# A LoRA router on one core: trip counter instead of an address test, the logits' wrap once per trip, spare products at other places

## The chip, the core and the metric

The kernel runs on one NeuronCore of a Trainium2 chip. The metric is the device time of one execution in microseconds; the time before is the median of three runs. The profile is of a separate execution of the same program, and times inside it count from its first instruction.

## The reference

```python
batch, seq, dim, num_loras = 16, 512, 1024, 8      # x: 16 x 512 x 1024 fp32
logits = np.matmul(x, router_weights)              # router_weights: 1024 x 8
exp_logits = np.exp(logits - np.max(logits, axis=-1, keepdims=True))
out = exp_logits / np.sum(exp_logits, axis=-1, keepdims=True)
```

A matrix of 8192 rows and 1024 columns is multiplied by 1024 x 8 weights, and each row's eight logits go through a softmax. Input is 33.55 MB, output 0.26 MB.

## The kernel before

**Blocks.** The 8192 rows are taken as 128 partitions of 64 rows, and block j is row j of every partition, so 128 rows of 1024 values. `x_all` holds all 64 blocks in SBUF in bf16 and no place in it is used twice; so a load never waits for the compute engines.

**Loads.** `LOADS` (line 40) is the list of loads in blocks: one of 4, four of 8, four of 4, three of 2, five of 1, which makes 63. The first, blocks 0 to 3, is issued by SyncE as fp32 into `x_f32` and cast by ScalarE (line 361). The others are issued by GpSimd, one after another (line 187), and are cast on the way. The loads of eight bring blocks 4 to 11, 12 to 19, 20 to 27 and 28 to 35. Block 63 comes last, in three pieces of 512, 256 and 256 columns (line 200). SyncE waits for each load in turn and adds its number of blocks to one semaphore, `s_in` (lines 170 to 175).

**TensorE.** [...] each block is first turned: eight 128 x 128 transposes against an identity, five into the PSUM tile `ptv` and three into `pts` (line 296 in the profile, since `loop_turn` copies the instruction written there; two tiles of each, used in turn). VectorE copies `ptv` to `xTv` (line 421), ScalarE `pts` to `xTs` (line 375). Then eight matmuls with the turned block as stationary operand and the bf16 weights as moving operand (128 x 8) accumulate a block's logits in `lg` (line 283 in the profile, copied from the spare product). Turns run one block ahead of products.

The order on TensorE is written out by hand as a loop of its own (lines 305 to 324). One trip handles two blocks: `rows_turn` turns an odd block (`loop_turn(1)`) and multiplies the even one before it; `rows_even` turns the next even block (`loop_turn(0)`); `rows_multiply` runs two spare products and multiplies the odd block. A spare product (`fill`, line 283) multiplies a constant tile of 512 columns into a PSUM tile that nobody reads; it keeps the array occupied. Each turn begins with a wait for `s_in` (line 232), each product with a wait for both copies of its block, `s_c` (line 262).

**Registers.** Eight registers `r_x` hold the address of the next block's eight column groups, and `r_l` the address of the logits in PSUM, 256 bytes further with each block. The ring of logits has 16 places of 256 bytes, so the address wraps at 4096: line 246 clears that bit after each addition. After each turn the additions stand in two fused register operations with that line between them (lines 243, 246, 247 in the profile). At the end of `rows_turn` lines 319 and 320 decide if spare products are inserted: some bits of the address of the next block are compared, which holds for blocks 12, 20, 28 and 36; the address of `x_all` (`ROW_AT`, line 57) is chosen so that these bits fall right. If it holds, `rows_spare` runs six spare products ahead of the turn of that block. Line 323 ends the trip and branches back to `rows_multiply`.

**After the loop.** Blocks 61 and 62 are multiplied, block 63 is turned by pieces (`turn_piece`, lines 332 to 337, each with its own wait) and multiplied (lines 346 to 354). The softmax of blocks 0 to 59 runs by groups of eight on VectorE and ScalarE beside the loop, that of the last four one by one (lines 366, 470, 524 to 531). SyncE stores blocks 0 to 59 and then the last four.

## Time and profile before

| | |
|---|---|
| time, median of 3 (all) | 85.59 us (85.55 to 85.71) |
| span of the profiled execution | 84.5 us |
| TensorE matmul, busy | 69.4 us (82%) |
| VectorE / ScalarE, busy | 39.4 / 38.0 us |
| spare products, 85 | 25.8 us, 401 ns each |
| turns in the loop, `ptv` + `pts` | 29.0 + 21.7 us |
| products in the loop, `xTv` + `xTs` | 16.7 + 13.2 us |
| granted TensorE clock, mean | 0.994 |
| GpSimd's loads: packets, bytes, share of 16 engines' span | 2736, 15.73 MB, 90.2% |

Matmuls overlap in the array, so their durations add up to more than the time that passes: a transpose is recorded with some 218 ns, but the next one starts 55 ns later. The bytes of a queue are counted as written, in bf16. PEq is TensorE's sequencer, which works through register operations, branches and waits; where the array waits for one, the line behind `<-PEq` names it. Line 232 is the wait for loaded blocks.

### The profile page before, as it was taken

To read this page: it belongs to the slowest core of one execution; us is meant where nothing else is said; L and a number is where in the kernel's file an instruction comes from. 1 tells how busy PE (TensorE), PEld (TensorE's weight loads), DVE (VectorE), ACT (ScalarE), POOL (GpSimd) and SP (SyncE) were. 2 spreads that over 40 slices of the span, in tenths; PEclk is the share of its full clock that TensorE was granted. 3 is DMA by queue.
4 is the path that set the end of the run, shared out by engine and by line. 5 is a ranking of instruction groups with operands and counts; after the bars stand their busy time and mean duration, and the time that the engine had idled before them with its cause. 6 is when DMAs were issued, how large, how long until landed. Compare 5 with 4: busy or idle time off the path is not lost. (4 is left out here: it accounts for less than half of the span.)

```text
span 84.5 us, 3030 instructions
## 1 busy us (share of the span) xinstructions
PE 69.4 (82%) x1118; PEld 54.2 (64%) x1118; DVE 39.4 (47%) x114; ACT 38.0 (45%) x81; POOL 11.3 (13%) x26
## 2 busy tenths in 40 slices
PE   0070366779999999979996999999999999999870
PEld 0040455659786787638882787678877888877650
DVE  0030042224563476427551476437657646765662
ACT  0600968223354265425442265426556544655570
POOL 0699996000000000000000000000000000000000
PEclk9999999999999999999999999999999999999997
DMA  5999979997999799989997999999999999999930
GB/s 165 402 434 248 248 155 225 241 241 155 233 241 225 163 241 241 217 171 241 241 217 159 217 217 217 217 213 221 202 233 190 215 211 215 201 210 210 164 114 11
DMA packets 3184, 18.12 MB, mean 215 GB/s; under 512 B 488, under 2 KB 1000, under 8 KB 2032
## 3 DMA queue, kind: packets, MB, share of 16 engines
q0 software_dynamic: 2736, 15.73, 90.2%
q1 hardware_dynamic: 432, 2.36, 7.3%
q10 hardware_dynamic: 16, 0.03, 0.1%
HBM read 33.59 MB, written 0.26 MB: 401 GB/s over the span
## 5 line engine op out<-in xcount | busy, mean ns | idle before, releaser
L421 DVE COPY xTv<-ptv 128x640 bf16<-128x640 bf16 x63 | 31.0, 492 | 33.1 <-PE ptv L296 28.0
L375 ACT COPY xTs<-pts 128x384 bf16<-128x384 bf16 x63 | 30.0, 476 | 35.5 <-PE pts L296 35.1
L296 PE MATMUL ptv<-identity,x_all 128*128 128x128 bf16 x311 | 29.0, 226 | 7.6 <-PEq L232 4.1
L283 PE MATMUL spare<-filler 128*128 128x512 bf16 x85 | 25.8, 401 | 0.1
L296 PEld LDWEIGHTS ptv<-identity,x_all 128*128 (+1 forms) x311 | 19.1, 100 | 9.7 <-issue 9.2
L296 PE MATMUL pts<-identity,x_all 128*128 128x128 bf16 x186 | 21.7, 228 | 0.0
L283 PEld LDWEIGHTS lg<-w_bf,xTv 128*128 128x128 bf16 x305 | 15.8, 99 | 8.0 <-issue 1.6
L283 PE MATMUL lg<-w_bf,xTv 128*128 128x8 bf16 x305 | 16.7, 167 | 0.0
L296 PEld LDWEIGHTS pts<-identity,x_all 128*128 x186 | 13.9, 103 | 0.0
L283 PE MATMUL lg<-w_bf,xTs 128*128 128x8 bf16 x183 | 13.2, 166 | 0.0
L283 PEld LDWEIGHTS spare<-filler 128*128 128x128 bf16 x85 | 6.1, 101 | 4.8 <-issue 0.6
L283 PEld LDWEIGHTS lg<-w_bf,xTs 128*128 128x128 bf16 x183 | 9.0, 96 | 0.0
L187 POOL DMA_DIRECT2D x_all<-in_x_dram x16 | 8.6, 600 | 2.2 <-POOLq L149 2.2
L361 ACT CAST x_all<-x_f 128x1024 bf16<-128x1024 f32 x4 | 4.0, 1044 | 5.0 <-ACTq L378 5.0
L290 PE MATMUL lg<-ident,w 8*128 8x8 f32 x8 | 1.0, 250 | 4.7 <-PEq L288 4.7
L290 PEld LDWEIGHTS lg<-ident,w 8*128 8x128 f32 x8 | 0.9, 197 | 4.7 <-issue 4.7
L441 DVE TENSOR_REDUCE mx<-lg 128x8 f32 x8 | 1.8, 225 | 4.4 <-DVEq L491 4.0
L412 DVE CAST identity<-ident 128x128 bf16<-128x128 f32 x1 | 0.5, 518 | 4.6 <-POOL ident L193 4.6
L364 ACT ACTIVATE ev<-ex 128x64 f32<-128x64 f32 x8 | 2.0, 256 | 1.4 <-DVE ex L441 0.8
L377 ACT ACT_TABLE_LOAD x1 | 1.3, 1283 | 2.2 <-PEq L149 2.2
L457 DVE TENSOR_REDUCE ssum<-ev 128x8 f32<-128x64 f32 x8 | 1.7, 218 | 0.0
L441 DVE TENSOR_TENSOR ex<-lg,mx 128x64 f32<-128x64 f32 x8 | 1.7, 216 | 0.0
(41 smaller groups left out, 16.0 us busy)
## 6 DMA issues: line engine op xcount, KB each, us to landing
x_all<-in_x_dram POOLq DMA_DIRECT2D x4, 2048.0 KB, 27.7
x_all<-in_x_dram POOLq DMA_DIRECT2D x4, 1024.0 KB, 51.7
x_f<-in_x_dram SPq DMA_DIRECT2D x1, 2048.0 KB, 8.4
x_all<-in_x_dram POOLq DMA_DIRECT2D x3, 512.0 KB, 62.1
x_all<-in_x_dram POOLq DMA_DIRECT2D x5, 256.0 KB, 66.2
out_dram<-out_all SPq DMA_DIRECT2D x1, 240.0 KB, 2.0
x_all<-in_x_dram POOLq DMA_DIRECT2D x1, 128.0 KB, 67.8
x_all<-in_x_dram POOLq DMA_DIRECT2D x2, 64.0 KB, 67.6
```

What stands on the lines that cost most here:

```text
L187: nc.gpsimd.dma_start(out=xa[:, first[i]:first[i] + r, :], in_=x_rows[:, first[i]:first[i] + r, :]).then_inc(s_ld[i], 16)
L283: return pe.matmul(spare, lhsT=filler[:, 0:P], rhs=filler, start=True, stop=True)
L290: t = pe.transpose(w_ps[:, n, :], w8[:, :, n], ident[0:KO, 0:KO])
L296: turn_like = pe.transpose(turn_ap(0, 0), xa[:, 0, 0:P], identity).ins
L361: act.copy(xa[:, k, :], x_f32[:, k, :]).then_inc(s_cast, 1)
L364: return act.activation(ev, ex, func=Exp).then_inc(s_ev, 1)
L375: act.copy(xTs[j % 2], pts[j % 2][:, 0:SN, :]).then_inc(s_c[j % 2], 1)
L377: act.preload_act_table(Exp)
L412: dve.tensor_copy(out=identity, in_=ident).then_inc(s_idb, 1)
L421: dve.tensor_copy(out=xTv[j % 2], in_=ptv[j % 2][:, 0:VN, :]).then_inc(s_c[j % 2], 1)
L441: return dve.add_instruction(kind(name=f"I-{nc.next_id()}", engine=dve.engine, **k))
L457: dve.reduce_sum(ssum[:, :, 0], ev, axis=X).then_inc(s_d, 1)
```

## The change

The test of address bits makes way for a counter. `r_t` starts at 1 and goes down by one in each odd turn, in the same fused operation as the addresses; when it falls below 1, the new `rows_wait` adds four (half of the eight blocks of a large load), and a second test asks if the next block lies below block 36, the end of the loads of eight. If so, the spare products run; if not, `rows_last` sets the counter so high that it doesn't return. There are five spare products in a group instead of six. The logits' address is wrapped in odd turns alone: it starts at place 3, so in even turns it can't reach the end of the ring. As no address bits are tested any more, `x_all` moves to the start of the free space, and `x_f32` behind it.

The aim is fewer register operations on TensorE's sequencer per trip, and no spare products where the loads are small.

```diff
-    LOT, SPARE = 8, 6
-    ROW_AT = 32 - LOADS[0] - LOT
-    assert LOADS[1:5] == [LOT] * 4 and 64 - ROW_AT == LOADS[0] + LOT * 5
+    LOT, SPARE = 8, 5
+    LOTS = LOADS.count(LOT)
+    assert LOADS[1:1 + LOTS] == [LOT] * LOTS
...
+    X_AT = place[0]
+    xa = sb("x_all", [P, J, D], bf16)
     x_f32 = sb("x_f32", [P, LOADS[0], D], fp32)
-    place[0] = X_AT = ROW_AT * D * 2
-    xa = sb("x_all", [P, J, D], bf16)
...
     pe.reg_mov(r_l, LG_AT + 256 * (SKIP - 1))
+    pe.reg_mov(r_t, 1)
...
         pe.reg_add(r_l, r_l, 256)
+        if b == 1:
+            pe.reg_add(r_t, r_t, -1)
         for c in range(KO):
-            if c == KO // 2:
+
+            if c == KO // 2 and b == 1:
                 pe.reg_alu(r_l, r_l, -4097, ALU.bitwise_and)
             pe.reg_add(r_x[c], r_x[c], D * 2)
...
     nc.br("rows_turn", engines=only_pe)
+
+    with nc.body("rows_wait", valid_engines=only_pe):
+        pe.reg_add(r_t, r_t, LOT // 2)
+        pe.br_lt(
+            r_x[0], X_AT + D * 2 * (LOADS[0] + LOTS * LOT),
+            on_true="rows_spare", on_false="rows_last",
+        )
+    with nc.body("rows_last", valid_engines=only_pe):
+        pe.reg_mov(r_t, J)
+        pe.br("rows_even")
     with nc.body("rows_spare", valid_engines=only_pe):
         for _ in range(SPARE):
             fill()
...
         multiply(0, None)
-        pe.reg_alu(r_t, r_x[0], (64 + 32 + LOT - 1) * D * 2, ALU.bitwise_and)
-        pe.br_eq(r_t, 32 * D * 2, on_true="rows_spare", on_false="rows_even")
+        pe.br_lt(r_t, 1, on_true="rows_wait", on_false="rows_even")
```

## The prediction

> **What bounds the kernel now.** I read the page first: the slices and the traffic.

> ```profile
> PE   0070366779999999979996999999999999999870
> ...
> DMA  5999979997999799989997999999999999999930
> ...
> HBM read 33.59 MB, written 0.26 MB: 401 GB/s over the span
> ```

> Both rows are full for most of the span: the DMA engines from about 2 us to slice 37, TensorE from about 21 us on, and busy shares cannot tell which sets the end. The wait that does is found in the timeline of TensorE (start, length, line, what it does, idle before it):

> ```profile
> 35.03 1.45 PE L283 MATMUL spare<-filler 128*128 128x512 bf16 x6
> 36.93 0.44 PE L296 MATMUL ptv<-identity,x_all 128*128 128x128 bf16 x5 [0.45 <-PEq L232]
> ...
> 44.37 1.46 PE L283 MATMUL spare<-filler 128*128 128x512 bf16 x6
> 46.60 0.44 PE L296 MATMUL ptv<-identity,x_all 128*128 128x128 bf16 x5 [0.78 <-PEq L232]
> ...
> 54.04 1.46 PE L283 MATMUL spare<-filler 128*128 128x512 bf16 x6
> 55.33 0.44 PE L296 MATMUL ptv<-identity,x_all 128*128 128x128 bf16 x5
> ...
> 79.70 0.44 PE L296 MATMUL ptv<-identity,x_all 128*128 128x128 bf16 x5 [0.40 <-PEq L232]
> ```

> These are the waits of line 232, for data: 0.45 us ahead of block 20, 0.78 ahead of block 28, then none for 33 us, then 0.40 ahead of block 62, the last whole block. So TensorE runs behind the loads from 46.6 us and catches up with them only at the end. The other side of that wait is SyncE's line 175, which counts each landed load:

> ```profile
> L175 SPq EVENT_SEMAPHORE  x16: 17/17/17, 17.3 to 79.5; - x16
> ```

> Cut into windows, its records stand at 17.3, 27.0, 36.8, 46.4 (loads of eight), 51.3, 56.1, 61.1, 65.9 (fours), 68.3, 70.8, 73.3 (twos), then 74.5, 75.7, 77.0, 78.3 and 79.5. A load of eight reads 8 x 128 x 1024 x 4 B = 4.19 MB in 9.7 us, 433 GB/s; the rate is the same late in the kernel (4.9 us per four). The pieces of block 63 land at 80.14, 80.49 and 80.90, and the weight load of the last piece's transposes starts at 80.94. From 80.90 to the span's end at 84.47 is a tail of 3.57 us: copy, product, softmax, store, none of it in the loop. **The end is the last landing plus 3.57 us, as long as TensorE is in time; it has 0.40 us in hand at block 62.** The chain of waits says the same: it begins at 79.66, with that block.

> [...] five transposes take 0.69 us until 21.2 us and 0.44 from 22.3 on. [...] the trace has 75 ns not taken and 207 taken, and I use those.

> **The change, part by part.** The sequencer's records of the lines concerned (ns, min/median/max):

> ```profile
> L246 PEldq ALU_OP  x62: 36/36/42, 10.8 to 79.9; - x62
> ...
> L319 PEldq ALU_OP  x31: 32/32/32, 11.5 to 79.0; - x31
> ...
> L320 PEldq COMPARE_BRANCH  x31: 75/75/207, 11.7 to 79.1; - x31
> ...
> L323 PEldq COMPARE_BRANCH  x31: 76/208/218, 13.7 to 80.1; - x31
> ```

> (1) *The wrap leaves the even turns.* In an even turn lines 243, 246, 247 and 323 start at 68.05, 68.17, 68.27 and 68.38; the taken branch ends at 68.59 and the next spare product's weights load at 68.65. The last transpose starts at 68.50 and one takes 0.055, so the array could have gone on at 68.56: a hole of 0.09 us per trip, caused by the sequencer. Dropping line 246 moves the branch up by 0.097 (its distance to line 247) and closes it: a trip goes from 1.83 (spare products at 68.65, 70.48, 72.31) to 1.74. Bounds: 0 and 0.10 per trip.

> (2) *The counter replaces line 319.* The decrement joins the fused register operation (64 ns with five additions, 60 with four: about 4 ns). Line 319, 0.09 to the next record, goes. Both are in the odd half, where the array shows no hole because the sequencer is ahead of it. Zero, hidden by the queued transposes.

> (3) *Spare products.* Six take 54.04 to 55.33, 0.215 each. Before, they stand ahead of blocks 12, 20, 28 and 36, 24 in all. After, r_t starts at 1, is 0 at the first test and is raised by 4: the groups of five fall when r_x[0] points to blocks 2, 10, 18, 26 and 34, 25 in all. So they come one trip (two blocks) earlier than the wait for the load of eight that they stood before; at block 42 the address is past 36 and r_t becomes 64, so that nothing follows.

> (4) *The detour.* Five times a taken branch, an addition, a second compare-and-branch: at most 0.1 + 0.2 us each[...]. Only the one at block 34 counts behind block 28: 0 to 0.3, I take 0.2. No semaphore wait is added anywhere.

> (5) *Addresses.* x_all moves from byte 40960 to 16640 of each partition and x_f32 behind it; loads, order and sizes stay. Cost zero: nothing in the trace ties the rate to the place, and x_f32 stood at 16640 before.

> Sum for TensorE: from block 28 at 46.60 to block 62 are 17 trips. Before 17 x 1.83 + 6 x 0.215 = 32.4, ready at 79.0 (79.3 observed). After 17 x 1.74 + 5 x 0.215 + 0.2 = 30.9, ready at 77.5. That is 1.5 us more in hand, and none of it gets into the end, since block 62 still lands at 79.5. It comes back as waits: at 1.74 a trip, block 48 is due at 65.3 but lands at 65.9, block 56 at 73.2 against 73.3, and blocks 60 to 62 each wait for their landings. In the tail the even turn of block 62 is 0.1 us shorter, ahead of pieces that land at 80.14 to 80.90; hidden too. The first half is cushioned likewise: five slow products (0.43 each) ahead of block 2 take 11.7 to 13.9, against 13.3 when block 2 starts now, and the 0.6 us vanish in the 1.04 us wait ahead of block 4. **Change at the end: 0.00 us, so 85.59.**

> **The rivals.** *Clock (slower).* With spare products gone from directly ahead of blocks 20 and 28, TensorE is done early: four trips of 1.74, 1.08 of spares and 0.2 after 36.93 make 45.2, so the idle stretch ahead of block 28 grows from 0.78 to 1.4 us, likewise ahead of 20. [...] A cold trip takes 2.98 us (spare products ahead, 17.50 to 20.48) instead of 1.74[...].

> *Loads slower.* If the new place of x_all costs the stream 0.4%, the end moves by 0.3: 85.9. [...]

> *Loads faster.* From 27.0 to 80.9 us the 44 blocks 20 to 63 take 53.9 us, where 9.7/8 = 1.21 each would make 53.3: 0.6 us are lost in the small loads at the end. If what loses them is the traffic of a TensorE that runs without pause, a TensorE that waits could give half back: 85.3. [...]

> *TensorE sets the end (faster).* If block 62 was in truth late for another reason than its landing, 0.4 us could be had: 85.2. Against it: line 175's record at 79.55 and the wait's at 79.60 lie together.

> **How the numbers follow.** No change 0.69 (85.45 to 85.75, the spread of the times before being 85.55 to 85.71). Clock 0.12, loads slower 0.05: slower 0.17. Loads faster 0.09, TensorE 0.05: faster 0.14. The range 85.3 to 85.95 takes in the nearer form of each rival[...].

> **What would show it.** Right: pieces landing at 80.9 again; the hole ahead of the two spare products gone, trips of about 1.74; groups of five ahead of blocks 2, 10, 18, 26, 34; longer waits of the turn ahead of 12, 20, 28, and new ones at 48 and 60 to 62. Wrong: transposes of 0.69 us per five after 22 us (clock), or a last landing away from 80.9 by more than 0.15 us (loads), or an end that moves though that landing doesn't (tail).

## The result, and the profile after

The changed kernel takes 86.73 us (86.23 to 86.99) against 85.65 (85.55 to 85.75): 1.0111 times the time before, 95% interval 1.0071 to 1.0152. No change had been forecast (0.00 us, with a range up to 85.95), so the forecast is wrong. The profile of the changed kernel, however, hardly differs where the forecast looked. Its slices and traffic on the page:

```profile
span 84.5 us, 2986 instructions
...
PE   0070389979994999859995999999899999999870
...
DMA  5999989998999899989998999999999999999920
...
HBM read 33.59 MB, written 0.26 MB: 401 GB/s over the span
```

The span is the same 84.5 us, and so is the stream of loads. The timeline of TensorE (start, length, line, what it does, idle before it) shows the groups and waits:

```profile
12.30 2.31 PE L285 MATMUL spare<-filler 128*128 128x512 bf16 x5 [0.36 <-issue]
...
27.23 0.44 PE L298 MATMUL ptv<-identity,x_all 128*128 128x128 bf16 x5 [1.17 <-PEq L231]
...
36.97 0.44 PE L298 MATMUL ptv<-identity,x_all 128*128 128x128 bf16 x5 [1.28 <-PEq L231]
...
46.64 0.44 PE L298 MATMUL ptv<-identity,x_all 128*128 128x128 bf16 x5 [1.20 <-PEq L231]
...
58.95 0.60 PE L285 MATMUL spare<-filler 128*128 128x512 bf16 x2
...
60.77 0.44 PE L298 MATMUL ptv<-identity,x_all 128*128 128x128 bf16 x5 [0.39 <-PEq L231]
...
79.75 0.44 PE L298 MATMUL ptv<-identity,x_all 128*128 128x128 bf16 x5 [0.41 <-PEq L231]
```

The five products stand ahead of block 2 (12.30), the waits ahead of blocks 12, 20 and 28 are 1.17 to 1.28 us, and all turns after 16 us take 0.44 us; the clock's record is full from 15.98 to 84.25 us (before: from 21.95 to 83.39). Block 62 starts at 79.75 after a wait, 0.05 us later than before. The last piece lands at 80.94 (before: 80.90), and the span ends at 84.51.

**The span does not hold the difference.** Each execution has a time and a span of its own. Their difference, called the rest below, is 1.32 us for the kernel before (median; 1.27 to 1.38 over all its executions) and 2.33 for the changed one (1.43 to 2.49): 1.0 us more, nearly all of the 1.08 us by which the times differ. (The spans of single executions are on record to 0.1 us, so a single rest is known to about 0.05.) The rest lies at the end. The record of the array's clock goes on behind the last instruction; in the profiled executions it stops at 86.03 us before and at 87.23 after, with spans that end at 84.47 and 84.51. In each of the twenty traces of this document it stops 0.23 to 0.24 us later than the measured time of the same execution, so the two move together.

Not every execution of the changed kernel has the long rest: of its 11 here (4 in this measurement, 7 in same_again below) nine have 1.97 to 2.49 us, one has 1.43 with a span of 84.8, and one has 1.45 with a span of 84.3 and a time of 85.75. Only one execution of each kernel left a trace, and neither of these two did.

What happens at the end is seen in the windows of the last microseconds, behind the last store. Before (columns: window, its length, busy us and count of TensorE's matmuls and weight loads, VectorE, ScalarE, GpSimd, clock, DMA share, GB/s):

```profile
83.50:85.00 1.50, 0.00 (x0) 0.00 (x0) 0.00 (x0) 0.00 (x0) 0.00 (x0) 0.50 0.07 11
85.00:87.00 2.00, 0.00 (x0) 0.00 (x0) 0.00 (x0) 0.00 (x0) 0.00 (x0) 0.74 0.00 0
```

The same windows after:

```profile
83.50:85.00 1.50, 0.00 (x0) 0.00 (x0) 0.00 (x0) 0.00 (x0) 0.00 (x0) 0.75 0.07 11
85.00:87.00 2.00, 0.00 (x0) 0.00 (x0) 0.00 (x0) 0.00 (x0) 0.00 (x0) 0.50 0.04 8
```

In the kernel before, nothing moves after the last instruction; in the changed kernel the DMA engines move 8 GB/s for 2 us there, which is 16 KB. In the trace's records that is one packet of 16384 bytes on queue 8, of the kind *instruction*, from 85.86 to 87.22 us; the record of the clock stops together with it. The kernel before has no such packet within or after its span. (Ahead of the first instruction every trace has six or seven packets of this kind with 8192 bytes, on queue 14; they are not meant below.) After its kind it is called the fetch below. So the question became what in the change brings this packet at the very end.

### The profile page after: what moved, and what is told of

Read it like the earlier page. It is cut to its first block, busy times and chain, and to the rows that moved or that the text cites. A ratio compares the mean times of both kernels' runs of the same rounds, so it can differ in the third digit from the quotient of the medians.

```text
span 84.5 us, 2986 instructions
## 1 busy us (share of the span) xinstructions
PE 67.8 (80%) x1119; PEld 53.7 (63%) x1119; DVE 39.5 (47%) x114; ACT 37.9 (45%) x81; POOL 11.3 (13%) x26
## 3 DMA queue, kind: packets, MB, share of 16 engines
HBM read 33.59 MB, written 0.26 MB: 401 GB/s over the span
## 5 line engine op out<-in xcount | busy, mean ns | idle before, releaser
L298 PE MATMUL ptv<-identity,x_all 128*128 128x128 bf16 x311 | 28.1, 221 | 8.7 <-PEq L231 5.1
L285 PE MATMUL spare<-filler 128*128 128x512 bf16 x86 | 26.3, 403 | 0.6 <-issue 0.4
L298 PE MATMUL pts<-identity,x_all 128*128 128x128 bf16 x186 | 20.9, 222 | 0.0
L285 PEld LDWEIGHTS lg<-w_bf,xTv 128*128 128x128 bf16 x305 | 15.3, 97 | 7.4 <-issue 0.5
L298 PEld LDWEIGHTS pts<-identity,x_all 128*128 x186 | 13.3, 99 | 0.0
```

Of the source, the lines that this page charges most:

```text
L285: return pe.matmul(spare, lhsT=filler[:, 0:P], rhs=filler, start=True, stop=True)
L298: turn_like = pe.transpose(turn_ap(0, 0), xa[:, 0, 0:P], identity).ins
```

## The experiments

All times are medians; "before" was measured beside each group on the same chip, at 85.61 to 85.69 us. The table has all results; the texts follow below. Spans and rests are medians over the executions of a kernel, while the last column is from its one trace.

| kernel | time us | ratio to before (95%) | span us | rest us (range) | fetch of 16 KB at |
|---|---|---|---|---|---|
| before | 85.65 | | 84.4 | 1.32 (1.27-1.38) | none |
| changed | 86.73 | 1.0111 (1.0071-1.0152) | 84.45 | 2.33 (1.43-2.49) | 85.86 |
| same_again | 86.41 | 1.0075 (1.0047-1.0102) | 84.3 | 2.04 (1.45-2.49) | 85.58 |
| places_back | 86.50 | 1.0098 (1.0083-1.0113) | 84.3 | 2.17 (2.07-2.31) | 86.23 |
| f32_behind | 85.75 | 1.0009 (1.0000-1.0018) | 84.4 | 1.31 (1.27-1.35) | none |
| wrap_odd_only | 85.86 | 1.0014 (1.0006-1.0022) | 84.4 | 1.48 (1.44-1.52) | none |
| counter_same_spares | 85.90 | 1.0028 (1.0020-1.0037) | 84.3 | 1.59 (1.55-1.63) | none |
| early_spares_old_test | 85.82 | 1.0020 (1.0009-1.0031) | 84.3 | 1.48 (1.44-1.53) | none |
| counter_start_2 | 85.94 | 1.0025 (1.0012-1.0038) | 84.35 | 1.60 (1.54-1.63) | none |
| no_group_at_2 | 85.98 | 1.0033 (1.0021-1.0045) | 84.4 | 1.58 (1.54-1.63) | none |
| only_group_at_2 | 86.44 | 1.0088 (1.0066-1.0110) | 84.35 | 2.00 (1.88-2.38) | 85.99 |
| only_group_at_2_ten | 86.14 | 1.0073 (1.0045-1.0101) | 84.8 | 1.34 (1.32-1.35) | 82.73 |
| early_clock | 85.79 | 1.0020 (1.0012-1.0028) | 84.3 | 1.50 (1.44-1.54) | none |
| block_2_held | 85.58 | 0.9996 (0.9988-1.0004) | 84.3 | 1.33 (1.27-1.37) | none |
| first_trip_straight | 86.10 | 1.0055 (1.0036-1.0074) | 84.6 | 1.50 (1.44-1.53) | none |
| first_jump_no_products | 85.86 | 1.0016 (1.0005-1.0026) | 84.4 | 1.48 (1.44-1.51) | none |
| old_test_group_at_2 | 86.01 | 1.0032 (1.0019-1.0045) | 84.4 | 1.58 (1.54-1.63) | none |
| one_move_more | 85.72 | 1.0008 (0.9991-1.0025) | 84.4 | 1.32 (1.28-1.37) | none |
| ten_more_at_the_end | 86.55 | 1.0116 (1.0100-1.0133) | 85.2 | 1.34 (1.32-1.36) | 83.14 |
| groups_of_three | 86.75 | 1.0140 (1.0114-1.0166) | 84.4 | 2.22 (2.12-2.58) | 85.54 |

### Program, places, or the session

The changed kernel again, unedited:

> The changed kernel again, unedited, taken in turns with the kernel before on one chip. Its profile has the same span as before (84.5 us) while its time is 1.1 us longer, so the time lies outside the span between the first and the last instruction, or belongs to the session in which it was taken. Theory program (something in the changed program costs 1 us outside the span): 86.7 against 85.6, span 84.5. Rival session (the chip or the hour, not the program): 85.6 against 85.6, or both alike. Rival clock or loads, as predicted beforehand: span 85.5 with a last landing later than 80.9 or turns of 0.69 us.

86.41 against 85.68: it is the program. Its profiled execution has the fetch again, 1.36 us after its last instruction (after 84.22 comes 85.58), as in the first one (1.35). One of its seven executions, however, took 85.75 us with a rest of 1.45.

The changed loop with the places of before:

```diff
-    X_AT = place[0]
-    xa = sb("x_all", [P, J, D], bf16)
     x_f32 = sb("x_f32", [P, LOADS[0], D], fp32)
+    place[0] = X_AT = 20 * D * 2
+    xa = sb("x_all", [P, J, D], bf16)
```

> The changed kernel with the buffers at the places that they had before (x_f32 at byte 16640, x_all at 40960); all of the loop is the changed one. Theory places (the move of x_all and x_f32 costs the microsecond): 85.6. Theory loop (counter, wrap, spare products, or the blocks of TensorE's program): 86.7, like the changed kernel. Span 84.5 in both.

86.50: it is not the move. And in the kernel before, `x_f32` behind `x_all` instead of ahead of it:

```diff
-    x_f32 = sb("x_f32", [P, LOADS[0], D], fp32)
     place[0] = X_AT = ROW_AT * D * 2
     xa = sb("x_all", [P, J, D], bf16)
+    x_f32 = sb("x_f32", [P, LOADS[0], D], fp32)
```

> The kernel before with one edit: x_f32 lies behind x_all as after the change, x_all stays at 40960. The loop is that of before. Theory places, if it is the place of x_f32, the first load's target: 86.7. Theory loop: 85.6, as before.

85.75, at most 0.2% more; its rest is that of before. The theory of places is gone.

The wrap alone, in the kernel before:

```diff
-            if c == KO // 2:
+            if c == KO // 2 and b == 1:
```

> The kernel before with one edit: the logits' address is wrapped in odd turns only. Test, spare products and places are those of before. Expected by the prediction's step 1: the hole of 0.09 us ahead of the two spare products of a trip closes, trips of 1.74 instead of 1.83 us, longer waits for loads, and no change of the end: 85.6. If the microsecond hangs on this part of the loop: 86.7.

85.86: neither of the two numbers. The span is unchanged (84.4), and TensorE's gain comes back as longer waits ahead of the loads, as the prediction had it. But the rest is 1.48 us in place of 1.32, a small step that none of the theories had.

### Which part of the loop

The counter with the spare products of before:

```diff
-    LOT, SPARE = 8, 5
+    LOT, SPARE = 8, 6
...
-    pe.reg_mov(r_t, 1)
+    pe.reg_mov(r_t, 6)
...
-            r_x[0], X_AT + D * 2 * (LOADS[0] + LOTS * LOT),
+            r_x[0], X_AT + D * 2 * (LOADS[0] + LOTS * LOT + 1),
```

> The changed kernel with the spare products of before: groups of six ahead of blocks 12, 20, 28 and 36 (r_t starts at 6, the bound is one block later). Counter, detour and the wrap in odd turns stay. Theory idle (the stretches without work right ahead of the loads let something fall that the profile does not show, the clock being the candidate): about 85.86, like the kernel with the odd wrap alone. Theory detour (the counter's blocks in TensorE's program cost the time): 86.5. Theory block 2 (the new group ahead of block 2 does): 85.86.

The old test with five products two blocks earlier:

```diff
-    LOT, SPARE = 8, 6
-    ROW_AT = 32 - LOADS[0] - LOT
+    LOT, SPARE = 8, 5
+    ROW_AT = 32 - LOADS[0] - LOT + 2
...
-            if c == KO // 2:
+            if c == KO // 2 and b == 1:
```

> The kernel before with the wrap in odd turns and its address test shifted by two blocks: groups of five ahead of blocks 10, 18, 26, 34, none ahead of block 2; no counter, no detour. Theory idle: 86.4 to 86.5, as the changed kernel. Theory detour: 85.86. Theory block 2: 85.86.

The changed kernel with the counter starting one trip later:

```diff
-    pe.reg_mov(r_t, 1)
+    pe.reg_mov(r_t, 2)
```

> The changed kernel with one number changed: r_t starts at 2, so that the groups of five stand right ahead of the loads of eight, at blocks 4, 12, 20 and 28, and none at 36. Theory idle: 85.7 to 85.9. Theory detour: 86.5 (four detours to the spare products, one to the end, instead of five and one). Theory block 2: 85.9.

And four trips later:

```diff
-    pe.reg_mov(r_t, 1)
+    pe.reg_mov(r_t, 5)
```

> The changed kernel with r_t starting at 5: groups of five ahead of blocks 10, 18, 26 and 34, none ahead of block 2. Theory idle: 86.5. Theory detour: 86.4 to 86.5 (one detour fewer). Theory block 2: 85.86.

They take 85.90, 85.82, 85.94 and 85.98. The theory of idle stretches asked for 86.4 in the second and the last and falls; the detour asked for 86.5 in the first, third and last and falls. What all four lack is the group ahead of block 2, and in none of their traces is the fetch. The third differs from the changed kernel in one constant. In it the first group runs 4 us later, while TensorE waits for the load of blocks 4 to 11. From the timeline of counter_start_2:

```profile
16.32 2.22 PE L285 MATMUL spare<-filler 128*128 128x512 bf16 x5
```

and from its windows behind the last store, which are empty like those of before:

```profile
85.00:87.00 2.00, 0.00 (x0) 0.00 (x0) 0.00 (x0) 0.00 (x0) 0.00 (x0) 0.74 0.00 0
```

So 0.5 us (against same_again) to 0.8 us (against the first measurement) hang on whether the first group comes ahead of block 2. These three counter kernels without it have 1.58 to 1.60 us of rest, 0.26 to 0.28 more than before; the wrap alone gives 0.16. That the same 0.26 us are also contained in the changed kernel's rest is not shown: its two executions with a short rest have 1.43 and 1.45.

### What about the group at block 2: its time, its clock, its products

Only that group, the others removed by a bound at block 4:

```diff
-            r_x[0], X_AT + D * 2 * (LOADS[0] + LOTS * LOT),
+            r_x[0], X_AT + D * 2 * LOADS[0],
```

> The changed kernel with the bound lowered to block 4, so that of the five groups only the one ahead of block 2 is left (five products; TensorE then waits longer for its loads). Theory block 2 (this group is what costs most of the change): 86.4 to 86.7. Rival (it costs only together with the early groups later on): 85.9.

The same with ten products (`LOT, SPARE = 8, 10`):

> The same with ten products in the one group instead of five, about 2.1 us more on a cold array. Theory delay (the time by which TensorE is late early on reaches the end in a way that the profile does not show): 1 to 2 us more than with five. Theory warm (it matters only that the array gets its full clock early, some 15 us instead of 21): the same as with five, about 86.5.

The one group alone gives 86.44, and its fetch is at 85.99. With ten it is 86.14: not 1 to 2 us more, as lateness would have it, nor the same, as the early clock would, but less. What differs is on the page of only_group_at_2_ten. The fetch falls into the span, at 82.73 us, so the rest no longer holds it (1.34), but it overlaps the last store:

```profile
q8 instruction: 1, 0.02, 0.1%
...
out_dram<-out_all SPq DMA_DIRECT2D x1, 16.0 KB, 2.1
```

The last column is the time from issue to landing. In the kernel before:

```profile
out_dram<-out_all SPq DMA_DIRECT2D x1, 16.0 KB, 1.4
```

From the last landing of a load to the span's end it is 4.25 us here instead of 3.57, and the slower store is all of that. In both kernels with the fetch the time is longer than before, by 0.8 us with it in the rest and by 0.5 us with it in the span.

only_group_at_2 also shows the prediction's first rival at work. Without groups ahead of the loads the clock does fall; from its timeline:

```profile
36.65 0.69 PE L298 MATMUL ptv<-identity,x_all 128*128 128x128 bf16 x5 [2.54 <-PEq L231]
```

Five transposes take 0.69 us instead of 0.44 at block 20, after an idle stretch of 2.54 us; the clock's record has the lower clock from 35.8 to 42.6 us, and the mean granted clock is 0.953 (before: 0.994). The span stays at 84.35 us (median) all the same.

Two edits of the kernel before were to separate lateness from an early full clock. Seven more products where TensorE waits for the first load:

```diff
     mult_like = fill().ins
+    for _ in range(7):
+        fill()
```

> The kernel before with seven more spare products where TensorE waits for the first load anyway (from about 6 to 9.5 us), so that the array gets its full clock before block 2 and nothing is delayed. Theory warm: 86.2 to 86.7. Theory delay: 85.65, as before.

And block 2 held back until block 3 is cast:

```diff
-        sp.wait_ge(s_cast, j + 1)
+        sp.wait_ge(s_cast, (1, 2, 4, 4)[j])
```

> The kernel before with block 2 held back until block 3 is cast (SyncE waits for four casts before it counts block 2), about 0.9 us later than now, with no spare product added. Theory delay: 86.2 to 86.5. Theory warm: 85.65, as before.

Block 2 started at 14.39 instead of 13.3 and the time did not move (0.9996): lateness by itself is not it. The other run did not do what it was made for: in its profiled execution the turns of blocks 2 and 4 still take 0.69 us, so the clock did not come early, and nothing follows for the clock. (It does show that seven products more in an idle place put 0.18 us into the rest.) The clock was answered by two later kernels, first_trip_straight and old_test_group_at_2: their clock is full from 12.9 and 13.7 us on in the profiled executions, earlier than in the changed kernel (16.0), and they have no fetch. So a full clock early on does not bring the fetch about by itself.

### What brings the fetch about

The five products at the same place, but without a branch to them, in the kernel before:

```diff
+    loop_turn(1)
+    multiply(0, None)
+    for _ in range(5):
+        fill()
-    nc.br("rows_turn", engines=only_pe)
+    nc.br("rows_even", engines=only_pe)
```

> The kernel before with its first half trip written out ahead of the loop: block 1 is turned, block 0 multiplied, five spare products follow, and the loop is joined at the turn of block 2. So the five products ahead of block 2 are there, but no branch leads to them. In all kernels with a group ahead of block 2 the trace has one more DMA packet, an instruction fetch of 16 KB on queue 8, that starts near or after the last instruction; in the others it is missing. Theory fetch by jump (the early jump back to the group's block brings the fetch about): no fetch, 1.3 to 1.6 us from the last instruction to the end, 85.6 to 85.9. Theory products: fetch, 2.0 to 2.4 us, 86.4. Theory length (how many instructions stand in the program): either.

The branch without products: only_group_at_2 with `SPARE = 0`:

> The changed kernel with no product in the groups and the bound at block 4: the counter still leads to the group's block in the first trip, which is empty. Theory fetch by jump: the fetch of 16 KB is there, 86.4. Theory products: no fetch, 85.9. Theory length: either, since the program is ten instructions shorter.

The old test with groups of six ahead of blocks 2, 10, 18 and 26, the program otherwise that of before:

```diff
-    ROW_AT = 32 - LOADS[0] - LOT
+    ROW_AT = 30
```

> The kernel before with its address test shifted so that the groups of six stand ahead of blocks 2, 10, 18 and 26. Program text and length as before, only constants differ. Theory fetch by jump and theory products: fetch, 2.0 to 2.4 us after the last instruction, 86.4. Theory length: no fetch, 85.6. Theory counter (only the new blocks bring it about): no fetch, 85.6.

A register move more, in the kernel before:

```diff
     pe.reg_mov(r_l, LG_AT + 256 * (SKIP - 1))
+    pe.reg_mov(r_t, 0)
```

> The kernel before with one dead register move ahead of the loop, about 0.09 us at a time when TensorE waits for data anyway. Theory length (also for the steps of 0.15 and 0.27 us in the time after the last instruction that the edits of TensorE's program showed): 85.75 to 85.9 with 1.5 us or more after the last instruction. Otherwise 85.65.

None of the four has the fetch. The products at that place don't bring it about without the jump (first_trip_straight), nor do the two together with the old test (old_test_group_at_2). All kernels in which it was seen have the counter's program and a group with products ahead of block 2.

first_jump_no_products says less than it was made for. Its trace lacks the branch that leads out of the group's block (line 322 of the changed kernel, five records there, one in only_group_at_2, none here): the empty block was evidently dropped ahead of the chip. So the jump to that block, the products in it and the branch out of it went together, and TensorE's program became shorter as well; which of them the fetch needs stays open.

first_trip_straight is longer for another reason: its span is 84.6, since its TensorE is late at the end. Block 62 lands at 79.29 us there and its turn starts at 79.64, behind block 61 and without a wait; from the last landing to the span's end it is 3.90 us instead of 3.57. The last of the four is void as a test of length: both traces have nine register moves, so the added one, whose value nobody reads, was dropped ahead of the chip, it seems; it only repeats the kernel before.

Last, two changes of the length. Five transposes behind TensorE's last product, into a tile no longer read:

```diff
     m.then_inc(s_p, 1)
+    for c in range(5):
+        pe.transpose(ptv[0][:, c, :], xa[:, 0, c * P:(c + 1) * P], identity)
```

> The changed kernel with five transposes added behind TensorE's last product, into a PSUM tile that nobody reads any more; TensorE has nothing to do there for 2.6 us, so in the span they cost nothing. Theory position (the fetch starts when TensorE's sequencer comes to a certain place of its program, and the ten more instructions bring it there before the last wait instead of after it): fetch at 82 to 84 us, as with ten products in the group (82.7), 1.3 us after the last instruction, and 85.6 to 86.2. Rival (something at the end of the execution starts it): fetch at 85.9, 86.5.

And groups of three products (`LOT, SPARE = 8, 3`):

> The changed kernel with three products in a group instead of five, at the same blocks 2, 10, 18, 26, 34: four instructions fewer in TensorE's program, the jump in the first trip stays. Theory position: the fetch comes later still or not at all, 1.5 to 1.6 us after the last instruction, 85.8 to 86.0. Theory jump (with products behind it): fetch at 85.9 and 86.5.

Ten instructions more at TensorE's end moved the fetch from 85.86 to 83.14 us, into the span. From the page of ten_more_at_the_end:

```profile
span 85.2 us, 2996 instructions
...
q8 instruction: 1, 0.02, 0.1%
```

The rest fell to 1.34 us, but the last store slowed down, by as much as the time from the last landing to the span's end grew (4.41 us instead of 3.57):

```profile
out_dram<-out_all SPq DMA_DIRECT2D x1, 16.0 KB, 2.2
```

The time stayed at 86.55. As only TensorE's program was edited, the fetch depends on what TensorE does, and not on the end of the execution alone.

Set beside only_group_at_2_ten, this says more. Five products more in the group and five transposes more at the end both make TensorE's program ten instructions longer, and in both the fetch starts 1.13 to 1.15 us after TensorE's last matmul (81.58 to 82.73, 82.01 to 83.14). In the five other traces with a fetch it starts 1.35 to 1.36 us after the last instruction of all engines, which is 4.0 us after TensorE's last one. That fits a place in TensorE's program which ten more instructions bring ahead of the wait for the other engines. Length alone does not decide, since counter_start_2 has the same program and no fetch. And fewer products in a group, four instructions less, did not put it off, as this theory had asked: it starts 1.35 us after the last instruction with three products as with five. If TensorE passes that place quickly behind its last wait, four instructions would hardly show; no run tests this.

**What stays open.** That the long rest is this fetch is shown: it is in the trace of every kernel with a median rest of 2 us or more and missing from the traces of all kernels with 1.3 to 1.6 that have none in their span; in the five traces with the fetch in the rest the record of the clock stops together with it, to 0.001 us; and where it is moved into the span, the excess moves with it. Why a first group ahead of block 2 is followed by a fetch 70 us later, while the same program with the group one trip later isn't, no run shows, nor why two of the changed kernel's 11 executions have a short rest. That queue 8 serves TensorE is not on record either; it is concluded from ten_more_at_the_end. Nor is it settled why the rest has steps of 0.16 and 0.26 us without any fetch: kernels with the wrap and the old test, with seven products more, with the first trip written out, or with the counter and an empty group have 1.48 to 1.50, the three other counter kernels without a fetch 1.58 to 1.60, and so has old_test_group_at_2, in which only constants differ from before.

None of these kernels beats the kernel before; block_2_held, one_move_more and f32_behind come out within 0.1% of it.

## Why the prediction was wrong, point by point

**The end of the span is the last landing plus 3.57 us.** Right: 80.94 + 3.57 = 84.51.

**The wrap (1).** Right in the span. The two spare products of consecutive trips start at 57.22 and 58.95, so 1.73 us for a trip (forecast 1.74). The sequencer's records (ns, min/median/max):

```profile
L331 PEldq COMPARE_BRANCH  x31: 76/76/235, 11.6 to 79.1; - x31
L334 PEldq COMPARE_BRANCH  x31: 69/201/207, 13.7 to 80.0; - x31
L311 PEldq ALU_OP  x6: 36/36/36, 11.9 to 60.1; - x6
L312 PEldq COMPARE_BRANCH  x6: 76/207/208, 12.0 to 60.2; - x6
```

The branch that ends a trip costs what it did (201 against 208), and the alone-standing operation ahead of it is gone. But the wrap alone does not reach this: in wrap_odd_only most trips take 1.74 or 1.75 us and every third or fourth 1.78 to 1.87.

**The counter (2).** Hidden in the span, as forecast, but not quite zero for TensorE: with the wrap and the counter together (counter_same_spares) trips without a group or a wait take 1.77 us at most, so the counter contributes. The fused operation grew by 10 ns, from 64 to 74, where 4 had been worked out.

**The spare products and the detour (3, 4).** The places were right. The detour at block 34, put at 0.2 us with 0.3 as the bound, costs about 0.26: its trip takes 3.07 us, against 1.73 and five products of 0.215. The first one leaves the array idle for 0.36 us, and block 2 starts at 14.40, where 13.9 had been worked out. The sixth detour, to the end of the counting, was not costed: it shows as 0.39 us ahead of block 42 (60.77 above), where the block had been loaded since 56 us, and its trip takes 2.37 us, 0.64 more than the others. All of it lies in TensorE's time in hand.

**The addresses (5).** Right within 0.2%: places_back and f32_behind.

**The waits that take the gain.** 1.17 to 1.28 us ahead of blocks 12 to 28 (1.4 forecast), 0.41 at block 62: TensorE's gain came back as waits. Blocks 48, 56, 60 and 61 start 0.15 to 0.16 us after SyncE's record of their landing, as block 62 does, so they wait for it too, as forecast. One sum was off: from block 48 at 65.9, four trips of 1.74 us make block 56 due at 72.9, not at 73.2, so its wait is a clear one.

**The rivals.** Clock: the changed kernel's profile has no turn of 0.69 us after 16 us, and its clock's record is full up to 84.25; where the clock fell ahead of block 28, in only_group_at_2 for 6.8 us, the fall was absorbed (span 84.35). A fall behind block 28 did not occur in the changed kernel; what it would have cost at the end is not shown. Loads, slower or faster: last landing 0.04 us later, no. TensorE as the bound: no.

**The step that failed** is the last of the sum, "Change at the end: 0.00 us, so 85.59". It takes the end of the span for the end of the execution. The numbers read at the start, 85.59 us and a span of 84.47, left 1.1 us that belong to no line of the page; the prediction carried them along as a constant and gave no rival for them. All four rivals move the loads or TensorE within the span, and so does the sign of being wrong that comes nearest, an end that moves though the last landing doesn't: it looks at the tail within the span, which stayed at 3.57 us. What the runs showed in place of the constant: the term was 1.32 us before and 2.04 to 2.33 after (medians), and it holds the change, 0.72 us of 0.73 in the second measurement and 1.0 of 1.08 in the first. The fetch makes up 0.45 to 0.75 us of that if the 0.26 us of the other counter kernels are in it as well, and all of it otherwise. That the span itself came out within 0.04 us is no luck: landings and tail behaved as the prediction had read them.

## What to carry to other kernels

Set the measured time against the profile's span before anything else, on both sides of a change: if the difference between the two moves, no line within the span will explain that part of the result, and the traffic behind the last instruction is the place to look, for DMA packets of the kind *instruction* above all. In this loop, which waits for its loads, the edit of the control flow saved about 0.1 us of TensorE's time per trip (1.83 to 1.73 us) and none of the span (84.47 and 84.51), while the time grew by 1.08 us together with a fetch behind the last instruction; so change the constant that decides when the first detour is taken, here r_t from 1 to 2 (86.73 to 85.94 us), and measure it as a variant of its own. The time freed on TensorE was worth nothing here: it came back as waits for loads, 1.17 to 1.28 us ahead of blocks 12 to 28.
